# Attention of the second block in units of two heads: weights normalised before the transposes, V stationary in column halves

## The chip, the cores and the metric

The kernel runs on one core of one Trainium2 chip. The metric is the time of one execution on the device in microseconds (us), the median over repeated runs. The engines are TensorE (PE, with its weight loads as PEld), VectorE (DVE), ScalarE (ACT), GpSimd (POOL) and SyncE (SP, which issues the DMAs). Each takes its instructions in the order of its own queue; semaphores hold an instruction back until what it reads or overwrites is ready.

## What is computed

Two blocks of a network over 256 tokens of 1024 channels, in fp32. The first block has two layers of a mixer (mLSTM and dilated attention) and a gated MLP. The second block takes the result as its latents, beside 256 tokens of context; its first layer mixes by attention with 16 heads of 64 channels (4 heads of keys and values, each shared by 4 heads of queries), a window and a sink, its second by gated linear attention. Only this attention matters here:

```python
def softmax_with_sink(s, sink):
    sk = sink.astype(jnp.float32)[None, :, :, None, None]
    m = jnp.maximum(jnp.max(s, axis=-1, keepdims=True), sk)
    e = jnp.exp(s - m)
    return e / (jnp.sum(e, axis=-1, keepdims=True) + jnp.exp(sk - m))
...
        p = softmax_with_sink(jnp.concatenate([s_lat, s_ctx], axis=-1), sink_g).astype(v.dtype)
        return (jnp.einsum('bhgqk,bkhd->bqhgd', p[..., :n_loc], v)
                + jnp.einsum('bhgqk,bkhd->bqhgd', p[..., n_loc:], v_ctx))
```

The latents attend to 256 latent keys (within the window) and 256 keys of the context, 512 in all; the context attends to its own 256 keys. The outputs of all heads, [256, 1024], go through `w_o`.

## The kernel before

Nearly all products are done as three fp32r products of high and low parts (`mm3`, L581; `mm_nat`, L620). The weights come as 591 tiles of [128, 1024], called granules (and 192 more for the adaLN vectors). `ahead` (L453) loads the granules to come (SyncE), makes their high parts `wh` (ScalarE) and low parts `wl` (VectorE), some granules ahead of TensorE. `gran` (L476) does the products of one granule and then one `tick`.

Background work is written as generators. `add` (L501) puts one on a list, with a delay in ticks; `tick` (L508) lets every generator on the list do one step, the oldest first. What a step issues goes into the queues there and then, and the program's order is kept on each engine. So two steps on one engine, in one tick, run in the order of the list, and a step that waits holds up all that stands behind it on its engine. `tick` with main also issues one product of the adaLN vectors (`ada_step`, L549: a multiply and reduction over [128, 1024] on VectorE, its weights loaded by a DMA of 512 KB), if the planner's account says that VectorE is ahead (`late`, L371, below `room`). The account (`Core`, L342) adds for a VectorE instruction 90 ns and its elements a partition divided by 0.96 per ns, and counts TensorE by the columns.

The attention runs in two stages. That of the **context** (`ctx_units`, L1711) runs as background of the first MLP of the first block, whose granules (the loop over `FF` in `layer1`) fill TensorE: 16 units of two heads (h0 and h0 + 2) for one of two query blocks, one unit for every three granules. That of the **latents** (`layer2_attention`, L1804, the loop from L1829) has 32 units of one head, one started at each tick. Eight granules of the context's MLP are put in between, at passes 1, 2, 4, 6, 12, 18, 24 and 30 of the loop; each brings a tick of its own. The last steps of `q_out`, for the last queries, fall into the first ticks.

A unit (`unit`, L1655) has six steps, one a tick, in one bank of PSUM:

1. scores, and the window's mask as a product (TensorE);
2. maximum over the keys and its negation `nm` (VectorE), exponentials `P` with their sum `den` (ScalarE);
3. transposes of P (TensorE); `es`, the sink's share, an addition on VectorE and an exponential on ScalarE;
4. copy of the transposed weights `PT` (ScalarE, or VectorE for every second head of the latents); `den + es` and its reciprocal (VectorE);
5. products with V, PT stationary (128 columns), V moving (64 columns): `aux<-v,PT` or `trb<-v,PT`;
6. the output times the reciprocal into `on` (VectorE for the latents, ScalarE for the context).

For every four heads, `o_out` (L1789) transposes `on` of both blocks (four transposes) and splits the result into high and low parts `oT`, the operand of the product with `w_o` (`aux<-wh,oT` for the latents). The banks of PSUM come from three pools: `mm` (2 banks), `aux` (4), `tr` (2, `trb`); the units of the latents take four of `aux`, then one of `tr`.

Of the kernel before, what the change touches and what calls it, by code (L numbers as in the profile page):

```python
# [18 lines left out]
T = 256  # L19
# [5 lines left out]
# columns of w_in  # L25
# [36 lines left out]
    # streams of the second block: 0 latents, 1 context, 2 both  # L62
# [128 lines left out]
# ------------------------------------------------------------------ small vectors, [128, n]  # L191
# [33 lines left out]
# ------------------------------------------------------------------ constants of the shapes  # L225
# the order of the first block's tokens: token % 4, token % 128 // 4, token // 128
# [33 lines left out]
def rope_tables():  # L260
    """[2, token, 256]: cosines, and sines with the sign of the rotation, for 4 heads of 64."""
# [9 lines left out]
def block2_masks():  # L271
    """window masks of the two query blocks [128, 2, 128], causal masks [128, 4, 128], scan resets [128, 2, 512]"""
# [36 lines left out]
class Views(list):  # L309
    """[128, 256] views of tiles; pair[n]: views 2n and 2n + 1 as one"""  # L310
# [6 lines left out]
class Lazy:  # L317
    """a sequence whose items are worked out when they are asked for"""
# [8 lines left out]
class Costs:  # L327
    """An engine whose instructions are counted in time, roughly"""
# [13 lines left out]
class Core:  # L342
    """The core, with a rough account of how far its tensor and vector engines are (in ns)."""
# [27 lines left out]
    @property  # L371
    def late(self):
        """how much work the vector engine has in front of it"""
        return self.dve - self.pe


class Kernel:
    LOAD, HI, LO, RAWS = 5, 3, 2, 4

    def __init__(self, ctx, tc, i, o):  # L380
# [11 lines left out]
        self.kv, self.on = [None, None], [None, None]  # L392
# [16 lines left out]
    # ---- tiles  # L409
# [25 lines left out]
    def t4x4(self, name, n=8):  # L435
        """n views [128, 2 (hi, lo), 256]; and the tiles [128, 2, 2, 256]"""
# [3 lines left out]
    def t4x8(self, name, n=8):  # L440
        """n views [128, 256]"""
# [3 lines left out]
    # ---- the stream of weights: loads and splits run ahead of the products  # L445
# [7 lines left out]
    def ahead(self, n):  # L453
        """loads, then the high parts, then the low parts of the granules to come"""
# [21 lines left out]
    def gran(self, key, mm, post=None):  # L476
        """One granule: its products, then a step of the background; post runs before the next granule's products."""
# [22 lines left out]
    # ---- background work: generators, one step a granule  # L500
# [34 lines left out]
    # ---- adaLN vectors, channels on partitions  # L535
# [1175 lines left out]
    def ctx_units(self):  # L1711
# [3 lines left out]
        for n, u in enumerate([(b, h0) for h0 in (0, 1, 4, 5, 8, 9, 12, 13) for b in range(2)]):  # L1715
            at = 2 + 3 * n
            self.add(self.unit(self.trb, 1, *u), at)
            if n % 4 == 3:
                self.add(self.o_out(1, n // 4, self.oc, self.trb), at + 8)
# [530 lines left out]
```

## Time and profile before

| | before |
|---|---|
| median of 3 runs | 2144.11 us (2143.8 to 2144.17) |
| profiled execution: span from first to last instruction | 2140.1 us |
| what lies around the span (median less span) | 4.0 us |
| TensorE busy | 2088.5 us, 98% |
| VectorE busy | 1581.5 us, 74% |
| ScalarE busy | 1156.2 us, 54% |
| mean granted TensorE clock | 0.994 of full |

The profile is one execution on the chip. A row of the timeline is: start us, duration us (of all merged ones together), engine, line, operation, output<-inputs by the program's names, shapes, count, and in brackets the idle time before it and what ended that. L338 is the line of a helper that records every instruction of TensorE and VectorE, so tiles tell them apart: `unm` is the unit's `nm`, `uden` its `den`, `ues` its `es`. Matmuls are pipelined, so their durations overlap, and the time that one takes of the engine is read from start to start. An fp32 product stands in the trace as two instructions. The granted clock 1.00 is TensorE's level of 2.4 GHz, 0.50 that of 1.2 GHz.

### The profile page before, as it was taken

The numbers are of one execution on the slowest core, as the hardware profiler recorded it, in microseconds if no ns is written. First come the engines' busy times: TensorE is split into PE (matmuls) and PEld (weight loads), VectorE is DVE, ScalarE is ACT, GpSimd is POOL, SyncE is SP. The second block draws the span as 40 slices with busy tenths as digits, with TensorE's granted clock in tenths as the row PEclk, the third lists the DMA queues.
The fourth block names the chain that finished last, engine by engine and source line by source line (L and its number), as shares of the span: only waits on it lengthen the run. The fifth ranks groups of instructions, "written<-read, shape, count | busy, mean of one in ns | idle before, by whom it ended". The sixth has DMA issues, their size and how long they took to land.

```text
span 2140.1 us, 38280 instructions
## 1 busy us (share of the span) xinstructions
PE 2088.5 (98%) x15192; PEld 1931.2 (90%) x15192; DVE 1581.5 (74%) x2681; ACT 1156.2 (54%) x1972; POOL 44.8 (2%) x62
## 2 busy tenths in 40 slices
PE   7999999999999999999999999999999999999998
PEld 6988999899998998999999998898998989877997
DVE  7778888788887988897899567786664485466555
ACT  5745665555555644666464455555542365445444
POOL 0000000000000000001000000000000010000000
PEclk9999999999999999999999999999999999999999
DMA  8776566688865777554589555304553253214553
GB/s 337 285 287 218 182 215 214 217 286 299 304 243 199 267 278 242 179 190 162 188 296 362 200 179 196 109 31 148 196 189 108 91 182 109 70 60 148 188 187 137
DMA packets 120883, 426.88 MB, mean 199 GB/s; under 512 B 13664, under 2 KB 18528, under 8 KB 120704
## 3 DMA queue, kind: packets, MB, share of 16 engines
q1 hardware_dynamic: 120704, 424.43, 57.0%
q8 instruction: 119, 1.95, 0.4%
q14 instruction: 60, 0.49, 0.1%
HBM read 423.33 MB, written 1.05 MB: 198 GB/s over the span
## 4 chain that ended last, share of the span: by engine, by line
PE 89%; DVE 5%; ACT 4%; issue 1%; DMA 0%; POOL 0%; DVEq 0%; POOLq 0%; SPq 0%; ACTq 0%
PE mm L338 54%; PE aux L338 29%; PE trb L338 5%; ACT wh L464 1%; DVE wl L338 1%; ACT xh L1461 0%; DVE yg L338 0%; ACT u L1499 0%; ACT u L896 0%; DVE hT L338 0%; DMA raw<-in_w 0%; ACT ah L905 0%; POOL rs L667 0%; DVE ee L338 0%; DVE mtmp L338 0%
## 5 line engine op out<-in xcount | busy, mean ns | idle before, releaser
L338 DVE TENSOR_TENSOR wl<-raw,wh 128x1024 fp32r<-128x1024 f32 x591 | 718.7, 1220 | 184.4 <-PE aux L338 72.5
L464 ACT ACTIVATE wh<-raw 128x1024 fp32r<-128x1024 f32 x591 | 623.6, 1059 | 366.5 <-PE mm L338 136.7
L338 PE MATMUL mm<-uT,wh 128*128 128x256 f32 x3488 | 633.2, 283 | 0.0
L338 PEld LDWEIGHTS mm<-uT,wh 128*128 128x128 f32 x3488 | 535.6, 189 | 3.0 <-ACT va L807 0.3
L338 PE MATMUL mm<-uT,wl 128*128 128x256 f32 x1744 | 489.4, 281 | 0.0
L338 PE MATMUL mm<-hT,wh 128*128 128x256 f32 x1888 | 340.5, 282 | 4.0 <-ACT y L1766 2.1
L338 PEld LDWEIGHTS mm<-uT,wl 128*128 128x128 f32 x1744 | 328.9, 189 | 0.0
L338 PEld LDWEIGHTS mm<-hT,wh 128*128 128x128 f32 x1888 | 292.9, 189 | 10.5 <-ACT y L1766 2.3
L338 PE MATMUL mm<-hT,wl 128*128 128x256 f32 x944 | 265.5, 281 | 0.0
L338 DVE CUSTOM_DVE_ANT_0 araw<-araw,silu 128x1024 f32<-128x1024 f32 x192 | 233.1, 1218 | 6.3 <-DMA araw<-in_w 3.8
L338 PE MATMUL aux<-wh,hid 128*128 128x512 f32 x640 | 199.6, 393 | 0.0
L338 PEld LDWEIGHTS mm<-hT,wl 128*128 128x128 f32 x944 | 178.4, 189 | 0.0
L338 PEld LDWEIGHTS aux<-wh,hid 128*128 128x128 f32 x640 | 117.9, 188 | 24.4 <-DVE hid L338 0.2
L338 PE MATMUL aux<-mlg,wh 128*128 128x256 f32 x704 | 129.6, 285 | 0.0
L338 PE MATMUL aux<-wl,hid 128*128 128x512 f32 x320 | 125.4, 392 | 0.0
L338 DVE TENSOR_TENSOR r<-r 128x256 f32<-128x256 f32 (+1 forms) x88 | 39.4, 448 | 116.1 <-ACT r L1899 116.0
L338 PEld LDWEIGHTS aux<-mlg,wh 128*128 128x128 f32 x704 | 109.5, 192 | 0.0
L1899 ACT ACTIVATE r<-mm 128x256 f32<-128x256 f32 (+1 forms) x88 | 35.8, 407 | 124.8 <-PE mm L338 124.8
L338 PE MATMUL aux<-mlg,wl 128*128 128x256 f32 x352 | 99.6, 283 | 0.0
L667 POOL TENSOR_TENSOR rs<-ve,mhalf 128x1 f32<-128x1 f32 (+1 forms) x48 | 41.3, 861 | 2078.0 <-DVE ve L338 1892.5
L338 PE MATMUL mm<-wh,hT 128*128 128x256 f32 (+1 forms) x352 | 78.9, 321 | 0.7 <-DVE qs L338 0.5
L338 DVE CUSTOM_DVE_ANT_0 junk<-araw,silu 128x1024 bf16<-128x1024 f32 x64 | 78.0, 1218 | 0.0
(367 smaller groups left out, 3140.5 us busy)
## 6 DMA issues: line engine op xcount, KB each, us to landing
raw<-in_w SPq DMA_DIRECT2D x591, 512.0 KB, 4.1
araw<-in_w SPq DMA_DIRECT2D x192, 512.0 KB, 5.2
abias<-in_abias SPq DMA_DIRECT2D x32, 192.0 KB, 4.9
xc<-in_ctx SPq DMA_DIRECT2D x4, 512.0 KB, 6.4
x<-in_x SPq DMA_DIRECT2D x2, 512.0 KB, 4.1
gb<-in_ln SPq DMA_DIRECT2D x2, 512.0 KB, 5.7
out_x<-x SPq DMA_DIRECT2D x4, 256.0 KB, 2.0
mk<-in_mmask SPq DMA_DIRECT2D x1, 512.0 KB, 5.5
```

The costliest lines, as they stand in the source:

```text
L338: return f(*a, **k)
L464: nc.scalar.activation(out=wh, in_=self.raws[self.nhi], func=AF.Copy)
L667: nc.gpsimd.tensor_tensor(out=rs, in0=ve, in1=self.mhalf[:, 0:n], op=ALU.pow)
L1899: nc.scalar.activation(out=r[:, 0:n], in_=ps, func=AF.Relu)
```

## The change

The attention of the second block is rewritten in units of two neighbouring heads, for latents and context.

- `weights` (new) does one head of the latents or two of the context: scores; maximum, exponentials and now also the sink's exponential, straight from `nm` on ScalarE; then, in a step of its own, `den + es`, reciprocal and the scaling of P (in place, on VectorE, 512 columns); then the transposes; then the copy of PT, always on ScalarE.
- `unit` runs `weights` for both heads, for the latents with the second head one tick behind the first one. Then come the products with V for both: V stationary (64 columns), PT moving (128 columns), the first head's output in partitions 0 to 63 of the bank, the second head's in 64 to 127. A last step splits this output, which is now transposed, straight into `oT`, 128 columns a unit.
- `o_out`, `on` and their transposes are gone.
- The units of the latents start at every second tick; their two banks come from `aux`, `aux`, `tr` in turn.

The rest of the diff takes out comments and empty docstrings.

```diff
+    def weights(self, bank, st, b, heads, res):
...
+        for n in range(step):
+            nc.scalar.activation(out=es[:, n:n + 1], in_=sink[:, n:n + 1], func=AF.Exp, bias=nm[:, n:n + 1])
+        yield
+        nc.vector.tensor_tensor(out=den, in0=den, in1=es, op=ALU.add)
+        nc.vector.reciprocal(out=den, in_=den)
+        for n in range(step):
+            c = slice(n * w, (n + 1) * w)
+            nc.vector.tensor_scalar(out=P[:, c], in0=P[:, c], scalar1=den[:, n:n + 1], scalar2=None, op0=ALU.mult)
         yield
         for k in range(4):
             nc.tensor.transpose(sc[:, k * 128:(k + 1) * 128], P[:, k * 128:(k + 1) * 128], self.ident)
-        nc.vector.tensor_tensor(out=es, in0=sink, in1=nm, op=ALU.add)
-        nc.scalar.activation(out=es, in_=es, func=AF.Exp)
         yield
         PT = self.t2("PT")
-        if st or h0 % 2:
-            nc.scalar.activation(out=PT, in_=sc, func=AF.Copy)
+        nc.scalar.activation(out=PT, in_=sc, func=AF.Copy)
+        res.append((sc, PT))
+
+    def unit(self, bank, st, b, h0, oT, made):
...
+        if st:
+            yield from self.weights(bank, st, b, heads, res[0])
+            yield
         else:
-            nc.vector.tensor_copy(out=PT, in_=sc)
-        nc.vector.tensor_tensor(out=den, in0=den, in1=es, op=ALU.add)
-        nc.vector.reciprocal(out=den, in_=den)
-        yield
-        for n, h in enumerate(heads):
-            vs = slice((h // 4) * 64, (h // 4) * 64 + 64)
-            vals = [kv[s]["v"][:, k, vs] for s in range(st, 2) for k in range(2)]
-            for k, v in enumerate(vals):
-                c = (n * len(vals) + k) * 128
-                nc.tensor.matmul(sc[:, n * 64:n * 64 + 64], PT[:, c:c + 128], v, start=k == 0, stop=k == len(vals) - 1)
-        yield
-        on = self.on[st][b]
-        for n, h in enumerate(heads):
...
+            parts = [self.weights(bank, st, b, [h], r) for h, r in zip(heads, res)]
+            next(parts[0])
+            yield
+            while not res[1]:
+                for p in parts:
+                    next(p, None)
+                yield
+        o = res[0][0][0][:, 0:128]
+        vs = slice((h0 // 4) * 64, (h0 // 4) * 64 + 64)
+        vals = [kv[s]["v"][:, k, vs] for s in range(st, 2) for k in range(2)]
+        for k, v in enumerate(vals):
+            for n in range(2):
+                PT, c = (res[0][0][1], (n * 2 + k) * 128) if st else (res[n][0][1], k * 128)
+                nc.tensor.matmul(o[n * 64:n * 64 + 64], v, PT[:, c:c + 128], start=k == 0, stop=k == len(vals) - 1)
+        yield
...
+        self.split(t[:, 0, bs], t[:, 1, bs], o)
...
     def layer2_attention(self, x, xc):
-        pools = (self.aux,) * 4 + (self.trb,)
-        left = [(0, b, hq) for hq in range(16) for b in range(2)]
-        for n, u in enumerate(left):
-            self.add(self.unit(pools[n % len(pools)], *u), n)
-            if n % 8 == 7:
-                self.add(self.o_out(0, n // 8, oT, self.trb), n + 7)
+        pools = self.aux, self.aux, self.trb
+        for n, u in enumerate([(b, h0) for h0 in range(0, 16, 2) for b in range(2)]):
+            self.add(self.unit(pools[n % 3], 0, *u, oT, made), 2 * n)
```

## Rows read from the trace of the kernel before

**Rows 1.** The first two parts of the page: busy time of the engines (share of the span, instructions), and TensorE's busy share in 40 slices of the span, in tenths.

```profile
PE 2088.5 (98%) x15192; PEld 1931.2 (90%) x15192; DVE 1581.5 (74%) x2681; ACT 1156.2 (54%) x1972; POOL 44.8 (2%) x62
...
PE   7999999999999999999999999999999999999998
```

**Rows 2.** Windows: stretch, its length, busy time of PE, PEld, DVE, ACT and POOL in it (instructions), granted clock, DMA share, GB/s. First from the context's stage, then from the latents'.

```profile
460.00:480.00 20.00, 20.00 (x172) 20.00 (x171) 18.18 (x36) 11.76 (x26) 0.00 (x0) 1.00 0.94 332
...
1402.00:1412.00 10.00, 10.00 (x80) 9.46 (x79) 8.67 (x30) 5.61 (x15) 0.00 (x0) 1.00 0.14 52
```

**Rows 3.** Timeline of TensorE in the latents' stage: transposes of P, scores, transposes of `on`, V products, transposes of P; a granule (from 1419.80 to 1422.61); the first output product.

```profile
1416.47 0.61 PE L338 MATMUL trb<-ident,P 128*128 128x128 f32 x4
1416.83 0.48 PE L338 MATMUL aux<-kT,qT 128*128 128x256 f32 x2
...
1417.50 0.60 PE L338 MATMUL trb<-ident,on 128*128 128x128 f32 x4
1417.94 1.00 PE L338 MATMUL aux<-v,PT 128*128 128x64 f32 x8
1418.78 0.61 PE L338 MATMUL aux<-ident,P 128*128 128x128 f32 x4
...
1419.80 0.63 PE L338 MATMUL mm<-wh,hid 128*128 128x512 f32 x2
...
1422.61 0.55 PE L338 MATMUL trb<-v,PT 128*128 128x64 f32 x4
...
1450.72 0.71 PE L338 MATMUL aux<-wh,oT 128*128 128x512 f32 x2
```

**Rows 4.** Timeline of VectorE, then of ScalarE, in the latents' stage, with nothing left out between the rows of either.

```profile
1408.36 0.69 DVE L338 TENSOR_REDUCE umx<-aux 128x1 f32<-128x512 f32 x1 [0.40 <-PE aux L338]
1409.08 0.16 DVE L338 SCALAR_TENSOR_TENSOR unm<-umx,nsink 128x1 f32<-128x1 f32 x1
1409.20 0.28 DVE L338 TENSOR_SCALAR on<-aux,uden 128x64 f32<-128x64 f32 x1
1409.40 0.15 DVE L338 TENSOR_TENSOR uden<-uden,ues 128x1 f32<-128x1 f32 x1
1409.58 0.17 DVE L338 RECIPROCAL uden<-uden 128x1 f32<-128x1 f32 x1
...
1409.36 0.69 ACT L1681 ACTIVATE P<-aux,unm 128x512 f32<-128x512 f32 x1 [0.45 <-DVE unm L338]
1409.94 0.19 ACT L1681 ACTIVATION_READ_ACCUMULATOR P<-aux,unm 128x1 f32 x1
1410.04 0.59 ACT L1691 ACTIVATE PT<-aux 128x512 f32<-128x512 f32 x1
1410.51 0.20 ACT L1687 ACTIVATE ues<-ues 128x1 f32<-128x1 f32 x1
```

**Rows 5.** Products of the second layer with a stationary operand of 64 columns (128*64), outputs in halves of the partitions: timeline of TensorE, and the weight loads of all of them (min, median and max ns).

```profile
1854.60 1.09 PE L338 MATMUL aux<-gS,gqk 128*64 128x256 f32 x8
1855.62 1.13 PE L338 MATMUL aux<-gv,ATm 128*128 128x256 f32 x4
1856.68 0.66 PE L338 MATMUL aux<-gS,gqk 128*64 128x256 f32 x4
...
L338 PEld LDWEIGHTS aux<-gS,gqk x64: 132/136/137, 1854.6 to 1919.7; 128*64 128x64 f32 x64
```

**Rows 6.** Timeline of TensorE around the V products of a unit of the context.

```profile
456.93 1.00 PE L338 MATMUL trb<-v,PT 128*128 128x64 f32 x8
457.73 0.48 PE L338 MATMUL aux<-mlg,wh 128*128 128x256 f32 x2
458.06 0.28 PE L338 MATMUL aux<-mlg,wl 128*128 128x256 f32 x1
458.17 0.40 PE L338 MATMUL aux<-mlg,wh 128*128 128x256 f32 x2
```

**Rows 7.** Groups of instructions by line, engine, operation, tiles and shape, count | busy us, mean ns | idle before: scalings by a column from SBUF to SBUF, and a copy of 128 columns on ScalarE.

```profile
L338 DVE TENSOR_SCALAR gon<-gon,rs 128x256 f32<-128x256 f32 x8 | 2.4, 348 | 0.8 <-POOL rs L667 0.8
L338 DVE TENSOR_SCALAR xh<-x,rs 128x1024 f32<-128x1024 f32 x8 | 6.0, 752 | 3.8 <-POOL rs L667 3.8
...
L1338 ACT ACTIVATE mD<-aux,gc 128x128 f32<-128x128 f32 x16 | 5.5, 362 | 0.3
```

**Rows 8.** The last adaLN products (by tile: min, median and max ns, first and last start), and the window behind them.

```profile
L338 DVE CUSTOM_DVE_ANT_0 araw<-araw,silu x4: 1217/1218/1219, 1172.2 to 1180.7; 128x1024 f32<-128x1024 f32 x4
...
1180.00:1200.00 20.00, 20.00 (x172) 20.00 (x171) 13.14 (x18) 8.95 (x12) 0.00 (x0) 1.00 0.55 184
```

**Rows 9.** The start of the latents' stage: timeline of VectorE, then a piece of the chain of waits (start us, us, what).

```profile
1361.60 0.68 DVE L338 TENSOR_REDUCE umx<-aux 128x1 f32<-128x512 f32 x1
...
1362.39 1.35 DVE L338 TENSOR_TENSOR rp<-qn,rope 128x512 f32<-128x512 f32 x3
...
1368.01 0.76 DVE L338 TENSOR_TENSOR qs<-qr,qs 128x256 fp32r<-128x256 f32 x2 [1.53 <-ACT qs L650]
...
1367.67 0.31 ACT qs L650
```

**Rows 10.** Timeline of TensorE with the idle time there, and a window of the latents' stage (granted clock third from the end).

```profile
1374.21 0.66 PE L338 MATMUL trb<-ident,qs 128*128 128x128 f32 x4 [1.56 <-ACT qT L1653]
...
1372.00:1382.00 10.00, 8.44 (x50) 7.58 (x49) 5.16 (x17) 5.13 (x13) 0.00 (x0) 0.83 0.16 54
```

More of the change, by code (lines that the diff above doesn't have):

```diff
@@ L391, in __init__ @@
         self.filler = iter(())
-        self.kv, self.on = [None, None], [None, None]
+        self.kv = [None, None]
         self.mix_filler = [self.ctx_qkv, self.ctx_in]
@@ L1653, in q_out @@
                 nc.scalar.activation(out=out, in_=src, func=AF.Copy)
-    def unit(self, bank, st, b, h0):
+    def weights(self, bank, st, b, heads, res):
         nc = self.nc
         kv = self.kv
-        step = 1 + st
-        heads = [h0 + 2 * n for n in range(step)]
+        step = len(heads)
         w = 512 // step
         bs = slice(b * 128, b * 128 + 128)
-        sink = self.V("sink")[:, h0:h0 + 2 * step - 1:2]
+        cs = slice(heads[0], heads[0] + step)
+        sink = self.V("sink")[:, cs]
         sc = bank()
@@ L1677, in unit @@
         nc.vector.tensor_reduce(out=mx, in_=sc.rearrange("p (a b) -> p a b", a=step), axis=AX.X, op=ALU.max)
-        nc.vector.scalar_tensor_tensor(out=nm, in0=mx, scalar=-1.0, in1=self.nsink[:, h0:h0 + 2 * step - 1:2], op0=ALU.mult, op1=ALU.min)
+        nc.vector.scalar_tensor_tensor(out=nm, in0=mx, scalar=-1.0, in1=self.nsink[:, cs], op0=ALU.mult, op1=ALU.min)
         P = self.t2("P")
@@ L1695, in unit @@
-        nc.vector.reciprocal(out=den, in_=den)
-        yield
-        for n, h in enumerate(heads):
-            vs = slice((h // 4) * 64, (h // 4) * 64 + 64)
-            vals = [kv[s]["v"][:, k, vs] for s in range(st, 2) for k in range(2)]
-            for k, v in enumerate(vals):
-                c = (n * len(vals) + k) * 128
-                nc.tensor.matmul(sc[:, n * 64:n * 64 + 64], PT[:, c:c + 128], v, start=k == 0, stop=k == len(vals) - 1)
-        yield
-        on = self.on[st][b]
-        for n, h in enumerate(heads):
-            if st:
-                nc.scalar.activation(out=on[:, h * 64:h * 64 + 64], in_=sc[:, n * 64:n * 64 + 64], func=AF.Copy, scale=den[:, n:n + 1])
-            else:
-                nc.vector.tensor_scalar(out=on[:, h * 64:h * 64 + 64], in0=sc[:, n * 64:n * 64 + 64], scalar1=den[:, n:n + 1], scalar2=None, op0=ALU.mult)
@@ L1711, in ctx_units @@
-    def ctx_units(self):
-        self.on[1] = [self.t4("on", (128, 1024)) for _ in range(2)]
-        self.oc = [None] * 8
[L1715 to L1719, printed above, removed]
+        nc.scalar.activation(out=PT, in_=sc, func=AF.Copy)
+        res.append((sc, PT))
+    def unit(self, bank, st, b, h0, oT, made):
+        nc = self.nc
+        kv = self.kv
+        heads = [h0, h0 + 1]
+        res = [[], []]
+        if st:
+            yield from self.weights(bank, st, b, heads, res[0])
+            yield
+        else:
+            parts = [self.weights(bank, st, b, [h], r) for h, r in zip(heads, res)]
[12 more added lines that the diff above has]
+                nc.tensor.matmul(o[n * 64:n * 64 + 64], v, PT[:, c:c + 128], start=k == 0, stop=k == len(vals) - 1)
+        yield
+        j = h0 // 2
+        if made[j // 2] is None:
+            made[j // 2] = self.t4("oT", (128, 2, 2, 256), F32R)
+        t = made[j // 2][:, j % 2]
+        bs = slice(b * 128, b * 128 + 128)
+        self.split(t[:, 0, bs], t[:, 1, bs], o)
+        if b == 1:
+            oT[j] = t
@@ L1721, in ctx_out @@
+    def ctx_units(self):
+        self.oc, made = [None] * 8, [None] * 4
+        for n, u in enumerate([(b, h0) for h0 in range(0, 16, 2) for b in range(2)]):
+            self.add(self.unit(self.trb, 1, *u, self.oc, made), 2 + 3 * n)
     def ctx_out(self):
@@ L1787, in tokens @@
         return lambda k, hl, b: a[k][:, hl, b * 128:(b + 1) * 128]
-    def o_out(self, st, j2, oT, bank):
-        nc = self.nc
-        on = self.on[st]
-        tr = bank()
-        for jj in range(2):
-            for b in range(2):
-                c = (j2 * 2 + jj) * 128
-                nc.tensor.transpose(tr[:, jj * 256 + b * 128:jj * 256 + b * 128 + 128], on[b][:, c:c + 128], self.ident)
-        yield
-        t = self.t4("oT", (128, 2, 2, 256), F32R)
-        nc.scalar.activation(out=t[:, :, 0], in_=self.pair(tr), func=AF.Copy)
-        nc.vector.tensor_tensor(out=t[:, :, 1], in0=self.pair(tr), in1=t[:, :, 0].bitcast(F32), op=ALU.subtract)
-        oT[2 * j2], oT[2 * j2 + 1] = t[:, 0], t[:, 1]
     def layer2_attention(self, x, xc):
@@ L1817, in layer2_attention @@
         self.flush()
-        self.on[0] = [self.t4("on", (128, 1024)) for _ in range(2)]
-        oT = [None] * 8
-        pools = (self.aux,) * 4 + (self.trb,)
-        left = [(0, b, hq) for hq in range(16) for b in range(2)]
-        for n, u in enumerate(left):
-            self.add(self.unit(pools[n % len(pools)], *u), n)
-            if n % 8 == 7:
-                self.add(self.o_out(0, n // 8, oT, self.trb), n + 7)
+        oT, made = [None] * 8, [None] * 4
+        pools = self.aux, self.aux, self.trb
+        for n, u in enumerate([(b, h0) for h0 in range(0, 16, 2) for b in range(2)]):
+            self.add(self.unit(pools[n % 3], 0, *u, oT, made), 2 * n)
         other = self.mlp_out(1, 1, self.hid_c, self.yc, self.mmb)
```

## The prediction

> **What bounds the kernel now.** Read first the busy line and the slices: TensorE is busy 98% of a span of 2140.1 us, VectorE 74%, ScalarE 54%, and TensorE's row of slices is all nines but for the first and last slice [rows 1]. So what the change takes from TensorE's queue is gained, unless another engine then ends last. The change lies in two stages, so the windows come next [rows 2]. In the context's stage (440 to about 620 us, between the granules of the first MLP) TensorE is busy 20.00 us of 20 and VectorE about 18. In the latents' stage (1358 to 1451 us) TensorE is full from 1402 us on, with VectorE at 8.7 us of 10, ScalarE at 5.6. The order of the queues says why. A tick of the latents' stage on TensorE is V products 0.84 us, transposes 0.36, scores and mask 0.67, 1.87 us a head, one right behind the other [rows 3]; VectorE waits for it (0.40 us ahead of a reduction) [rows 4]. The stage ends where the output product starts, at 1450.72 [rows 3].
>
> **The change, TensorE.** The transposes of `on` go: 32, four of them 0.44 us [rows 3], 16 in each stage, 1.75 us a stage. The V products get V as the stationary operand, 64 columns wide, in halves of the array. 128 columns of fp32 stream in 0.11 us (the transposes), 256 then in 0.22. The nearest row is gS<-gqk: eight half-wide products of 256 columns, 1.76 us one after the other, took 1.02 [rows 5], so two halves run side by side. Entering and leaving that form costs about 0.3 us together: eight of them and four full-wide ones, 8 x 0.22 = 1.76 us with the halves paired, took 1.02 + 1.06. A unit of the latents then has 8 pairs of 128 columns: 8 x 0.11 + 0.3 = 1.18 us for two heads, where 2 x 0.84 = 1.68 stand now; bounds 0.88 (no switching) and 1.76 (no pairing). A unit of the context has 4 pairs: 0.44 + 0.3 = 0.74 us. Now it takes 0.80, and the second product behind it starts 0.09 late (0.33 us for two, where one takes 0.11 to 0.12) [rows 6], 0.89; the gain is 0.15 a unit, 2.4 us for 16 (bounds 0 and 7).
>
> The Trainium skill ("TensorE: Matmul & The Clock Gate", Part 3) speaks against this part: weight loads overlap running matmuls only when the row group differs, and the halves here share their rows. By that rule a pair would cost its load and its stream. The gS rows contradict it: eight loads of 0.136 us and eight streams lie within 1.02 us [rows 5].
>
> **The context's stage.** TensorE gains 1.75 + 2.4 = 4.2 us. VectorE: out go `es` (0.15), and a quarter of the 0.69 us split of `oT`; in come two scalings of 256 columns, 0.35 each [rows 7], and a 128-column split, about 0.28: +0.66 us a unit, 10.6 us. The planner counts that (two scalings of 357 ns, one split of 223 by its formula, less `es` and the old split: +0.69 us a unit) and puts off some 9 adaLN products of 1.22 us instead. These ended at 1180.7 us with TensorE full and VectorE at 13 of 20 us in the next window [rows 8]; so they and their loads of 512 KB land there at no cost; if that cover were gone, 9 x 1.22 = 11 us. The new wait (the sum of the weights, on VectorE, one granule behind ScalarE's exponentials) has behind it an adaLN product and a split of weights, 2.4 us, in which the 1.1 us of exponentials end. Nothing else is late: **-4.2 us**.
>
> **The latents' stage, where I see the trouble.** Call a head's steps S (scores), M (maximum on VectorE, exponentials on ScalarE), N (sum, reciprocal and scaling of P on VectorE), T, C (copy of the transposes), V. Before, the reciprocal is two ticks behind M and touches only the output. Now N is in the tick right behind M and T waits for it. Units start every second tick with their heads one tick apart, older units first, so every tick puts on VectorE: N of one head, then the maximum of the next. N waits for the exponentials of the tick before; behind it in the same queue stands the maximum that the next exponentials wait for. That is a ring with one head in it: maximum, exponentials, N, maximum. From rows, start to start: reduction 0.72, negation to the start of the exponential 0.28, exponential 0.58, its sum 0.10, the sink's exponential 0.20, addition 0.18, reciprocal 0.20 [rows 4], and 0.03 from ScalarE's end to VectorE's start [rows 9]. The scaling of 512 columns has no row; 256 take 347 ns and 1024 take 753 [rows 7], so about 0.48, of which the last 0.08 overlap the next instruction as in [rows 4]: 0.40 (bounds 0.27 and 0.67, by those two rows). Sum 2.69 us a head, against 1.87 + 0.4 of granules now. In every second tick the split of an older unit stands ahead of N: its ScalarE half waits behind the exponentials (128 columns, about 0.33 by the 362 ns of mD [rows 7]), its VectorE half 0.20 more: 0.44 once the overlap is off.
>
> What hides in the ring's waits: wl (1.22 us, in the 1.2 us while VectorE waits for the exponentials), wh, both PT copies (2.69 - 0.89 = 1.8 us of each round are free on ScalarE), the 2.81 us granules (TensorE's share is 1.18 + 2 x 1.04 = 3.3 us a pair of heads and 0.8 of granules, 4.1 of 5.8), and the scores of a unit's second head, which wait for a bank until an older unit's outputs are split. What does not: the rotations of the last queries (1.35 us for three of four instructions, about 2.0), and their splits, for which VectorE waits 1.5 us [rows 9], some 2.5 us beyond the wait; a wh of 1.05 ahead of the split twice, 1.9; the additions to y, 0.8. So from the first reduction at 1361.60 [rows 9]: 1.91 to the first N, 31 x 2.69 = 83.4, 13 x 0.44 = 5.7, extras 5.2: the last N begins at 1457.8. Then N 0.9, T 0.5, C 0.6, V 1.2, the last granule 2.8: the output product starts at 1463.8, not 1450.72, **+13.1 us**. The 16 x 0.50 + 1.75 = 9.75 us that TensorE sheds here are off the path.
>
> **The clock.** Up to 1374.21 TensorE idled 1.56 us, and the mean granted clock of 1372 to 1382 is 0.83, which is 3.4 us at the lower level, 1.2 GHz (0.17 x 10 / 0.5) [rows 10]. TensorE will now idle some 1.7 us of every 5.8 (two heads, 2 x 2.69 + 0.44). Half the clock doubles 4.1 us a pair to 8.2, but only while it lasts, and the ring leaves TensorE slack. Bounds 0 and +15 us; I take +2, nearest to the one dip shown: 3.4 us at half the clock do the work of 1.7, of which the ring hides part.
>
> **The sum.** Span 2140.1 - 4.2 + 13.1 + 2 = 2151.0; the profiled span is 4.0 us below the median of the runs, 2144.1, so 2155.
>
> **Rivals.** *The ring does not bind* (faster). If the engines slip against each other as they do now, TensorE sets the pace: 9.75 us off in this stage, 4.2 in the other, 2130.1. It decides where a head's ring is below TensorE's 2.05 us (4.1 a pair); 2.3 us would make it even. For it: VectorE's own work, 1.6 to 1.9 us a head, is below 2.05, and TensorE is the bound now. Against: the waits are in a fixed order, and the terms are read off running queues. *Ring and gain cancel*: terms of the ring 0.3 us too large (a cheaper scaling, less of the extras), 2140 to 2148. *The clock stays low* for half of the stage: TensorE needs 6.2 us a pair beside a ring of 5.8 and each holds the other up, +8 to +15 more, 2162 to 2172. *The halves do not pair* (the change does not do what it says): the context's 2.4 us are lost, the latents hang on the ring, 2157.4. *Loads of the halves are not hidden*: a pair takes 0.136 + 0.11 us, a context unit 4 x 0.25 + 0.3 = 1.3, 0.4 more than now, 16 x 0.55 = 8.8 us above my sum; a latents' unit 2.3, still beside the ring: 2163.9. (That is the rule of Part 3 above.) *The put-off adaLN products collide*: up to +11, 2166.
>
> **How the numbers follow.** The ring as summed (with the halves pairing or not): 0.53, 2148 to 2162. Clock or adaLN on top: 0.15, to 2172; loads not hidden 0.02. Cancel: 0.10. Ring does not bind: 0.20, 2126 to 2140. 0.2% (4.3 us) is about what a measurement of this kernel tells from no change: faster 0.20, same 0.10, slower 0.70. The range from 2131 to 2168 leaves out about 0.1 at either end.
>
> **What would show it.** In the latents' stage of the changed kernel: VectorE idle about 1.1 us ahead of the additions to `uden`, released by ScalarE's `ues`, some 30 times; reductions 2.7 and 3.1 us apart in turn; TensorE idle ahead of the transposes of P, released by VectorE; half-wide products two at a time. In the context's stage: no idle TensorE, fewer adaLN products, the end of the stage some 4 us earlier. I am wrong if TensorE stays full in the latents' stage, or if reductions come closer than 2.3 us on the mean.

## The result

The changed kernel takes 2164.95 us, median of 4 runs (2164.16 to 2166.53), against 2144.11: ratio 1.0102, 95% interval 1.009 to 1.0115, so slower by 20.8 us. The forecast was 2155.0, in a range of 2131 to 2168. The direction, the mechanism and its pace were right; the loss is about twice the forecast one of 10.9 us.

The profiled execution has a span of 2164.7 us (before: 2140.1). The page of the changed kernel, busy line and two rows of slices (compare [rows 1]):

```profile
PE 2095.1 (97%) x15160; PEld 1919.6 (89%) x15160; DVE 1589.3 (73%) x2673; ACT 1164.0 (54%) x1996; POOL 44.6 (2%) x62
...
PE   7999999999999999999999999889999999999998
...
PEclk9999999999999999999999999899999999999999
```

The row of all nines has got two eights, at 1353 to 1461 us, and the clock's row one in the same stretch: the latents' stage. Windows of the changed kernel (columns: busy us of each engine, then granted clock, DMA share, GB/s):

```profile
1180.00:1200.00 20.00, 20.00 (x171) 20.00 (x170) 18.19 (x28) 8.81 (x11) 0.00 (x0) 1.00 0.94 343
1362.00:1372.00 10.00, 7.48 (x38) 5.63 (x36) 7.21 (x20) 4.45 (x11) 0.00 (x0) 0.82 0.17 58
1372.00:1382.00 10.00, 6.78 (x22) 5.61 (x23) 5.47 (x14) 5.30 (x13) 0.00 (x0) 0.50 0.14 53
1402.00:1412.00 10.00, 6.86 (x46) 5.45 (x45) 6.25 (x19) 5.65 (x18) 0.00 (x0) 0.84 0.01 2
1462.00:1472.00 10.00, 8.21 (x44) 6.15 (x45) 3.56 (x10) 4.20 (x10) 0.00 (x0) 0.60 0.16 51
```

The first row is the context's part: the adaLN products that were put off fill 1180 to 1200, VectorE 18.2 us where 13.1 stood [rows 8], and TensorE stays full beside them. In 1402 to 1412 no engine is full: TensorE 6.9 us of 10 (before 10.00 [rows 2]), VectorE 6.3, ScalarE 5.7. Each engine waits for another. VectorE's timeline there (start, duration, instruction, idle time before it and what ended that):

```profile
1404.07 0.68 DVE L338 TENSOR_REDUCE umx<-aux 128x1 f32<-128x512 f32 x1
1404.79 0.16 DVE L338 SCALAR_TENSOR_TENSOR unm<-umx,nsink 128x1 f32<-128x1 f32 x1
1406.04 0.16 DVE L338 TENSOR_TENSOR uden<-uden,ues 128x1 f32<-128x1 f32 x1 [1.09 <-ACT ues L1684]
1406.23 0.16 DVE L338 RECIPROCAL uden<-uden 128x1 f32<-128x1 f32 x1
1406.43 0.48 DVE L338 TENSOR_SCALAR P<-P,uden 128x512 f32<-128x512 f32 x1
1406.84 0.68 DVE L338 TENSOR_REDUCE umx<-aux 128x1 f32<-128x512 f32 x1
1407.55 0.16 DVE L338 SCALAR_TENSOR_TENSOR unm<-umx,nsink 128x1 f32<-128x1 f32 x1
1408.99 0.29 DVE L338 TENSOR_TENSOR oT<-aux,oT 128x128 fp32r<-128x128 f32 x1 [1.28 <-ACT oT L650]
1409.20 0.15 DVE L338 TENSOR_TENSOR uden<-uden,ues 128x1 f32<-128x1 f32 x1
...
1409.98 0.68 DVE L338 TENSOR_REDUCE umx<-aux 128x1 f32<-128x512 f32 x1
```

This is the ring as forecast: maximum, a wait of 1.09 us for the exponentials, N, next maximum; 2.77 us later in this pair and 3.14 where a split stands ahead of N (forecast 2.69 and 3.13). Those two spacings alternate from the seventh maximum to the last, but for three longer ones of 4.1. In two of these a split of weights (`wh`) stands ahead of the high half on ScalarE; in the third (1412.74 to 1416.89) a unit's V products stand behind a granule on TensorE:

```profile
1410.57 1.05 PE L338 MATMUL mm<-wh,hid 128*128 128x512 f32 x2
...
1414.45 1.09 PE L338 MATMUL trb<-PT,v 128*64 128x128 f32 x16
```

The start and the end are where the forecast is off. VectorE at the start of the stage, from the first maximum on:

```profile
1359.94 0.68 DVE L338 TENSOR_REDUCE umx<-aux 128x1 f32<-128x512 f32 x1
...
1367.53 0.76 DVE L338 TENSOR_TENSOR qs<-qr,qs 128x256 fp32r<-128x256 f32 x2 [1.99 <-ACT qs L650]
...
1378.66 0.69 DVE L338 TENSOR_REDUCE umx<-trb 128x1 f32<-128x512 f32 x1 [0.74 <-PE trb L338]
1379.39 0.16 DVE L338 SCALAR_TENSOR_TENSOR unm<-umx,nsink 128x1 f32<-128x1 f32 x1
1384.40 0.29 DVE L338 TENSOR_TENSOR oT<-aux,oT 128x128 fp32r<-128x128 f32 x1 [4.85 <-ACT oT L650]
```

The wait of 4.85 us goes back to TensorE, in the same execution:

```profile
1378.42 1.05 PE L338 MATMUL mm<-wh,hid 128*128 128x512 f32 x2
...
1382.63 0.39 PE L338 MATMUL mm<-wl,hid 128*128 128x512 f32 x1
1382.95 1.09 PE L338 MATMUL aux<-PT,v 128*64 128x128 f32 x16
```

A granule takes 4.5 us (2.81 in [rows 3]) because the clock is at its lower level, 1.2 GHz, until 1382; the first unit's V products stand behind it, the split behind those, and on VectorE N and the next maximum behind the split. The last maximum (VectorE), then TensorE at the end:

```profile
1461.99 0.68 DVE L338 TENSOR_REDUCE umx<-aux 128x1 f32<-128x512 f32 x1
...
1462.22 0.63 PE L338 MATMUL aux<-ident,P 128*128 128x128 f32 x4 [1.08 <-DVE P L338]
...
1464.65 1.97 PE L338 MATMUL trb<-PT,v 128*64 128x128 f32 x14 [1.44 <-ACT PT L1696]
1466.55 1.12 PE L338 MATMUL aux<-ident,P 128*128 128x128 f32 x4
1467.60 2.78 PE L338 MATMUL aux<-PT,v 128*64 128x128 f32 x16
1470.31 1.22 PE L338 MATMUL mm<-wh,hid 128*128 128x512 f32 x2
...
1474.96 0.63 PE L338 MATMUL aux<-wh,oT 128*128 128x512 f32 x2
```

From the last maximum (1461.99) to the output product it is 13.0 us, with V products of 2.7 us and a granule of 4.65, again at the lower level (0.60 in the window); the forecast had 7.9.

### The profile page after: what moved, and what is told of

It reads as the page before. It is cut to its first block, busy times and chain, and to the rows that moved or that the text cites. A ratio compares the mean times of both kernels' runs of the same rounds, so it can differ in the third digit from the quotient of the medians.

```text
span 2164.7 us, 38194 instructions
## 1 busy us (share of the span) xinstructions
PE 2095.1 (97%) x15160; PEld 1919.6 (89%) x15160; DVE 1589.3 (73%) x2673; ACT 1164.0 (54%) x1996; POOL 44.6 (2%) x62
## 4 chain that ended last, share of the span: by engine, by line
PE 85%; DVE 7%; ACT 5%; issue 1%; DMA 0%; POOL 0%; ACTq 0%; DVEq 0%; POOLq 0%; SPq 0%
PE mm L338 54%; PE aux L338 27%; PE trb L338 4%; DVE wl L338 1%; ACT wh L464 1%; DVE umx L338 1%; ACT P L1681 1%; DVE P L338 1%; DVE uden L338 0%; ACT xh L1461 0%; ACT u L896 0%; DVE yg L338 0%; ACT u L1499 0%; DMA raw<-in_w 0%; DVE hT L338 0%
```

## The experiments

Ratios are to the kernel before, run beside it on the same chip (medians of it 2142.65 to 2144.02). N is the sum, reciprocal and scaling of a head; a granule is one of the eight of the context's MLP between the latents' units.

**1. Maximum ahead of N.** N is put in a list that the tick runs at its end; the latents' instructions are the same, in another order.

```diff
-        nc.vector.tensor_tensor(out=den, in0=den, in1=es, op=ALU.add)
...
+        def norm():
+            nc.vector.tensor_tensor(out=den, in0=den, in1=es, op=ALU.add)
...
+        if st:
+            norm()
+        else:
+            self.ends.append(norm)
         yield
```

In `tick`, behind the steps of all generators:

```diff
+        for f in self.ends:
+            f()
+        self.ends = []
```

> The changed kernel, with the same instructions in another order: in each tick of the latents' stage the sum, reciprocal and scaling of a head (N) are issued behind the next head's maximum, not ahead of it. Theory (ring): maximum, exponentials, N, next maximum no longer follow one another for each head; TensorE sets the pace at about 3.9 us a pair of heads (2 x 1.03 us of scores and transposes, 1.03 of half-wide V products, 0.8 of granules) in place of 5.9, the low clock goes with the waits, and the stage gives back 25 to 37 us: 2128 to 2140 us, the output product at about 1438 to 1450, reductions 2.0 to 2.3 us apart on the mean, VectorE's wait for ues gone. Rival (the half-wide V products and the low clock at the ends of the stage are what costs): the order hardly matters, 2158 to 2166. Rival (VectorE's own work, 1.6 to 1.9 us a head, is the next bound and its waits stay): 2140 to 2150.

2139.01 us, ratio 0.9979 (0.997 to 0.9988): 26 us back by order alone, 4 of them at the end (9.0 us in place of 13.0), so the ring with the clock that it costs is the loss. VectorE in the steady part:

```profile
1423.26 0.29 DVE L338 TENSOR_TENSOR oT<-aux,oT 128x128 fp32r<-128x128 f32 x1 [0.49 <-ACT oT L653]
1423.46 0.68 DVE L338 TENSOR_REDUCE umx<-aux 128x1 f32<-128x512 f32 x1
1424.18 0.16 DVE L338 SCALAR_TENSOR_TENSOR unm<-umx,nsink 128x1 f32<-128x1 f32 x1
1424.26 0.15 DVE L338 TENSOR_TENSOR uden<-uden,ues 128x1 f32<-128x1 f32 x1
1424.44 0.16 DVE L338 RECIPROCAL uden<-uden 128x1 f32<-128x1 f32 x1
1424.64 0.49 DVE L338 TENSOR_SCALAR P<-P,uden 128x512 f32<-128x512 f32 x1
```

The wait ahead of the sum is gone; maxima come 1.58 and 2.36 us apart, 3.94 a pair, with 2.1 to 3.3 at granules; with the start they are 2.55 apart on the mean of the stage, where 2.0 to 2.3 was expected. The wait of 0.49 us for a split's high half is what is left.

**2. and 3. One stage alone.** The unit, the output transposes and the call of the kernel before serve the other stage.

> The change in the context's stage alone; the latents' attention is that of the kernel before. Theory: TensorE is the bound there and sheds 1.75 us of transposes and about 2 us of V products: 2139.5 to 2142.5 us (4.2 us by the forecast, 1.6 by what is left of it in the changed kernel when the latents' stage begins). Rival (the context's part is lost elsewhere, to the adaLN products that it puts off or to the clock): 2143.5 or more.

> The change in the latents' stage alone; the context's attention is that of the kernel before. Theory: the whole loss is here, 25 us by the trace of the changed kernel: 2166 to 2170 us. Rival (the stage is late because the context's part moved work into it): below 2160.

Context alone 2139.85, 0.9989 (0.9979 to 0.9999); latents alone 2165.51, 1.01 (1.0085 to 1.0115). The context's gain is 3.7 us by the medians (forecast 4.2), but the ten runs of 2 lie between 2139.27 and 2144.96, and the interval leaves room for 0.2 to 4.5. The whole loss is the latents'; its time is just below the expected range.

**4. Scores twice.**

```diff
-        for n, h in enumerate(heads):
+        for n, h in [e for e in enumerate(heads) for _ in range(2 - st)]:
             lhs = kv[st]["q"][h // 4][:, h % 4, bs]
```

> The changed kernel, with the score products of every latents' head issued twice over (the second time over the first, the same sums): 0.67 us a head, 21 us of TensorE work more, on an engine that waits for VectorE. Theory (ring, with the low clock at the start and the end of the stage on top): TensorE has 5.2 us of work in 5.9 a pair, so the ring's pace of 2.76 and 3.15 us stays; the busier engine keeps the full clock over more of the stage and the start and the end give back 3 to 10 us: 2155 to 2163. Ring, with the clock as a bystander: 2164 to 2168. Rival (TensorE's time counts, waits come and go): 21 us on top or a good part of them, 2175 to 2186.

2162.97, 1.0088 (1.0073 to 1.0103): 21 us of TensorE work more, and no more time. The pattern stays at 2.76 and 3.15; the granted clock is 1.00 from 1382 on, and the end takes 9.0 us (1461.60 to 1470.58) in place of 13.0. The start is no shorter: spacings of 5.47, 5.20 and 6.53, where the changed kernel has 5.47, 4.14 and 6.73.

**5. and 6. A later start.** Experiment 6 is the changed kernel with this edit, 5 has the order of 1 as well.

```diff
-            self.add(self.unit(pools[n % 3], 0, *u, oT, made), 2 * n)
+            self.add(self.unit(pools[n % 3], 0, *u, oT, made), 2 * n + 4)
-            if n in (1, 2, 4, 6, 12, 18, 24, 30):
+            if n in (1, 2, 3, 4, 16, 22, 28, 34):
```

> The order of e1_max_first, and beside it the first units of the latents begin four ticks later, with the first four granules of the context's MLP (2.8 us each at the full clock) in the four iterations ahead of them and the later four granules as far behind the units as before. In e1 the first six maxima lay 22.3 us apart in all, where 3 pairs of 3.95 us and two granules would be 17.5; TensorE idled beside the rotations and splits of the last queries, and its clock fell. Theory (those steps stand in the engines' queues among the first units'): the granules cover them, 4 to 8 us less than e1: 2131 to 2135 us. Rival (the start is bound by the queries' own chain of steps, which is no shorter): 2137 to 2142.

> The changed kernel with that later start alone; its ring stays. Its first nine spacings of maxima were 8.5 us longer than the ring's pattern by the trace (3.59, 5.47, 4.15, 6.73 us where 2.76 and 3.15 are the pattern), where the forecast had 2.5. Theory (the start of the stage is the mis-sized term): 4 to 8 us less than the changed kernel: 2157 to 2161 us, with the pattern of 2.76 and 3.15 from the third maximum on. Rival (the first units are slow by themselves): 2163 to 2167.

5: 2134.09, 0.9957 (0.9943 to 0.9972), as expected. 6: 2163.09, 1.0088 (1.0071 to 1.0105), where 2157 to 2161 was expected. In 6 the pattern does hold from the third maximum on, and first to last maximum is 93.7 us in place of 102.05; but the first maximum comes at 1366.30 in place of 1359.94, since two more granules (5.6 us), which stood among the units, are now ahead of it. The collisions of the start are real, 8.3 us; only the cover was not free.

**7. No scaling.** The loop over the scalings runs over `range(step if st else 0)`.

> The changed kernel without the scaling of the latents' weights by the reciprocal (left out: the attention of the latents is not normalised). Theory (ring): the scaling holds VectorE 0.40 us, start to start, in each head's round, and the round is the stage's pace, so maxima come 2.36 and 2.75 us apart and 31 x 0.40 = 12.4 us go: 2151 to 2154 us, a little less if the clock dips less. Rival (the wait for the exponentials takes the place of the scaling, because ScalarE or TensorE ends last): 2160 to 2166.

2146.68, 1.0016 (1.0006 to 1.0025). Maxima 2.25 and 2.61 apart: a round is 0.51 to 0.54 us shorter, since the scaling's wait for the reciprocal goes too. 31 x 0.52 is 16 us, and the clock, 1.00 from 1382 on, gives the end back. One term of the ring taken out shortens every round, so ring it is; the miss is that I counted 0.40.

**8. V products not in turn.**

```diff
-        for k, v in enumerate(vals):
-            for n in range(2):
+        for n in range(2):
+            for k, v in enumerate(vals):
```

> The changed kernel with the half-wide V products of a unit in another order: all of the first head, then all of the second, where they stood in turn. Theory (halves run side by side only when neighbours in the queue take different column halves): a context unit streams 8 x 0.11 where 4 x 0.11 stood, 0.44 us more, and the context's stage is bound by TensorE: 16 x 0.44 = 7 us more; the latents hang on the ring and hide theirs: 2169 to 2173 us, and a block of V products of the latents takes 1.8 to 2.1 us in place of 1.03. Rival (the halves do not run side by side now, or the engine finds the partner further down the queue): 2164 to 2167 and no change of the block.

2159.80, 1.0077 (1.0062 to 1.0092), below the range of either theory. Latents, not in turn, then the changed kernel, in turn (the starts of the transposes behind them are 1457.12 and 1457.27):

```profile
1455.60 1.58 PE L338 MATMUL aux<-PT,v 128*64 128x128 f32 x16
1457.12 0.66 PE L338 MATMUL aux<-ident,P 128*128 128x128 f32 x4
```

```profile
1456.24 1.09 PE L338 MATMUL aux<-PT,v 128*64 128x128 f32 x16
1457.27 0.66 PE L338 MATMUL aux<-ident,P 128*128 128x128 f32 x4
```

1.52 us and 1.03: the order matters there, and the latents hide it. In the context a unit's block takes 0.59 us from its start to that of the next instruction in either order, so there it does not, and the 7 us never came. The starts of the single instructions, not in turn, say more. The 16 of a latents' block fall into two rows of eight, 0.11 us apart within a row; the second row begins 0.49 us into the block, 0.006 us behind the fifth start of the first. In the context (two rows of four) it begins 0.01 us behind the first start. The trace does not name the heads; read as first and second head, a product starts beside one of the other half that stands four places ahead of it in the queue, and the latents' 0.49 us are the first four, alone. That the kernel became faster goes with the clock: 1.00 in 1462 to 1472, and an end of 9.0 us.

**9. A granule behind the V products.** `if n in (1, 2, 5, 6, 13, 19, 25, 31):` in the changed kernel: five of the eight granules move by one pass.

> The changed kernel with six of its eight granules of the context's MLP one iteration later or earlier, so that a granule stands behind a unit's V products in TensorE's queue and not right ahead of them. In the changed kernel the first unit's V products stand behind a granule that takes 4.5 us at half the clock; the first split waits for them, and with it everything behind the split in VectorE's queue: a spacing of maxima of 6.73 us in place of 3.15. Theory (that granule holds the ring): the spacing falls to 3.2 to 4 us and the kernel takes 2 to 4 us less: 2161 to 2163.5 us. Rival (the wait moves to the next granule): 2164 to 2167.

2159.49, 1.0077 (1.0064 to 1.009), below the expected range. VectorE at the first split:

```profile
1381.04 0.29 DVE L338 TENSOR_TENSOR oT<-aux,oT 128x128 fp32r<-128x128 f32 x1 [1.06 <-ACT oT L650]
```

1.06 us of waiting in place of 4.85; the spacings of 4.14 and 6.73 are 3.08 and 4.08, 3.7 us together. The end is 11.3 us in this execution, with a granted clock of 0.70 in 1462 to 1472 (0.60 in the changed kernel).

**10. to 12.** 10 is 5 with the later granules at 17, 23, 29 and 35. 11 is the kernel before with the edit of 5 (units at `n + 4`, output transposes at `n + 11`). 12 is 5 with the edit of 8.

> The order and the later start of e5_max_first_late, with the four later granules one iteration further, behind a unit's V products. Theory (a split that waits for a granule holds VectorE for 0.7 to 1.7 us, four times): 1 to 3 us less than e5, 2131 to 2133 us. Rival (TensorE is the bound, 9.5 us of 10, and the order of its work is all one): 2133.5 to 2135.

> The kernel before with the later start alone (its units four ticks later, the first four granules ahead of them): what of e5's gain is not the change's. TensorE idles 1.56 us and loses 1.7 us to the low clock at the start of the stage in the kernel before. Theory (the start costs both kernels much the same): 3 to 5 us less than before, 2139 to 2141 us, so that the change in its other order is worth some 5 to 7 us. Rival (only the changed kernel's order collides there): 2143 to 2145.

> e5_max_first_late with the V products of a unit not in turn: all of the first head, then all of the second, 1.51 us a block where 1.02 us stand in turn (the two as measured in the latents' stage of e8_not_in_turn and of the changed kernel). Theory (without the ring TensorE sets the pace of the latents' stage): all of 16 x 0.49 = 7.8 us come on top of e5: 2140 to 2143 us. Rival (VectorE and the splits still set it, or half of it): 2134 to 2138.

10: 2132.92, 0.9951 (0.9937 to 0.9964), not to be told from 5, and the fastest version tried. 11: 2137.00, 0.997 (0.9958 to 0.9982), more than the 3 to 5 us expected: the start costs the kernel before as much, so more than half of 10's gain is not the change's. 12: 2135.93, 0.9964 (0.995 to 0.9977), 1.8 us more than 5 where TensorE as the bound would give 7.8, and not to be told from 5. Its pattern is 1.58 and 2.36 as in 5. So the pace of 3.94 is not TensorE's, though there is no more room: from 1382 to 1432 TensorE is busy 10.00 us of 10 in 12. VectorE in 5:

```profile
1384.20 0.29 DVE L338 TENSOR_TENSOR oT<-aux,oT 128x128 fp32r<-128x128 f32 x1 [0.49 <-ACT oT L653]
1384.41 0.68 DVE L338 TENSOR_REDUCE umx<-aux 128x1 f32<-128x512 f32 x1
...
1388.15 0.29 DVE L338 TENSOR_TENSOR oT<-trb,oT 128x128 fp32r<-128x128 f32 x1 [0.49 <-ACT oT L653]
```

Between these rows VectorE waits only there: 3.45 us of work and 0.49 of wait a pair.

**13. and 14. The split's low half last.** The low half goes into a list that the tick runs behind N; 13 in the changed kernel, 14 in 10.

```diff
-        self.split(t[:, 0, bs], t[:, 1, bs], o)
+        hi, lo = t[:, 0, bs], t[:, 1, bs]
+        nc.scalar.activation(out=hi, in_=o, func=AF.Copy)
+        low = lambda: nc.vector.tensor_tensor(out=lo, in0=o, in1=hi.bitcast(F32), op=ALU.subtract)
+        if st:
+            low()
+        else:
+            self.lows.append(low)
```

> The changed kernel with one move: the low half of a split (VectorE) is issued at the end of its tick, behind the next maximum, not at the tick's head. Theory (the split is a term of the ring, since VectorE waits there for its high half on ScalarE): the spacing of 3.15 us falls to 2.76, 15 x 0.39 = 5.9 us, and where a granule or a split of weights delayed the split (6.73, 4.1 us) up to 6 us more: 2153 to 2160 us. Rival (the banks, which come free with the split, hold the scores back by as much): 2163 to 2167.

> e10_both (maximum first, later start, granules behind the V products) with the low half of the split last in its tick as well. In e5 a pair of heads takes 3.94 us, 3.45 of VectorE's work and 0.49 of its wait for the split's high half, and the pattern stayed at 3.94 with 0.49 us more on TensorE. Theory (VectorE with that wait is the bound once the ring is broken): up to 0.49 us a pair less, 3 to 7 us: 2126 to 2130 us. Rival (TensorE and the banks are as late; 9.6 us of 10 busy): 2131.5 to 2134.

13: 2160.87, 1.0084 (1.0068 to 1.0099), just above the expected range. The spacings are 2.76 and 2.78, so the split's 0.39 us is a term of the ring; but some rounds are longer (5.71, 4.16), and the start is as it was (4.14, 6.60). 14: 2143.72, 0.9999 (0.9991 to 1.0008): the theory fell. TensorE in 14:

```profile
1385.41 0.47 PE L338 MATMUL aux<-kT,qT 128*128 128x256 f32 x2 [1.62 <-DVE oT L338]
...
1390.49 0.48 PE L338 MATMUL trb<-kT,qT 128*128 128x256 f32 x2 [1.62 <-DVE oT L338]
```

The bank comes free with the low half, and the scores of a second head, which wait for it, are now 1.62 us late: 5.09 us a pair. The rival had named the banks, but priced them at 2131.5 to 2134.

**15. Scores four times** in the heads 0 and 1, twice in the others.

> The changed kernel with the score products issued four times over for the first four heads and twice for all others: TensorE is given work where it idles at the start of the stage (1.9, 2.3 and 1.0 us) and its clock falls. Theory (the low clock is 3 us of the start's excess, the queues the rest): full clock from 1362 to 1392, the spacing of 6.73 us down to 4.5 to 5.5 us, the spacing of 5.47 as it is, the end as in e4: 2158 to 2161 us. Rival (the start is order alone): the spacings stay and 2162 to 2165.

2163.61, 1.0097 (1.0083 to 1.011). Its windows:

```profile
1372.00:1382.00 10.00, 7.64 (x46) 6.89 (x46) 5.83 (x15) 4.75 (x11) 0.00 (x0) 0.83 0.17 55
1462.00:1472.00 10.00, 8.18 (x73) 6.34 (x73) 4.99 (x13) 5.09 (x14) 0.00 (x0) 1.00 0.16 52
```

With a granted clock of 0.83 in 1372 to 1382 in place of 0.50 the start is no shorter: spacings of 5.48, 5.21 and 6.04, and 27.3 us for the first six in place of 25.5 (the scores themselves add to some). So a higher clock alone does not mend the start. The end is 9.0 us again (1463.24 to 1472.22).

**16. and 17.** 16 is 11 with the context's part of the change. 17 is 14 with the low half between the maximum and N.

> The change in the context's stage alone, with the later start of e11_before_late: the latents' attention is that of the kernel before. Theory (the two add up, and the latents' part of the change is worth nothing even in its best order so far): 2137.0 - 3.7 = 2133.3, so 2132 to 2134.5 us, the time of e10_both. Rival (the latents' part in e10 is worth some us): 2135 or more.

> e14_all_three with the low half of a split between the next maximum and N, where e10_both has it ahead of the maximum and e14 behind N. Theory (VectorE's wait of 0.49 us for the high half is what sets 3.94 us a pair in e10, the bank held 1.6 us too long what set 5.1 in e14): the high half is ready when the maximum is done, VectorE does not wait, the bank comes free 0.3 us later than in e10: 3.45 to 3.7 us a pair, 4 to 8 us less than e10 over 16 pairs less what the granules take back: 2126 to 2130 us. Rival (the banks hold the scores back still): 2132 to 2140.

16: 2136.96, 0.997 (0.9958 to 0.9981), in the rival's range. With the later start the context's part shows no gain by the medians (11 has 2137.00), and 10 is some 4 us faster than either; the intervals of 10 and 16 still overlap a little. The profiled executions do not put those 4 us into the latents' stage. The output product starts, in 10, 16 and 11:

```profile
1442.89 0.62 PE L338 MATMUL aux<-wh,oT 128*128 128x512 f32 x2
1443.10 0.71 PE L338 MATMUL aux<-wh,oT 128*128 128x512 f32 x2
1445.96 0.71 PE L338 MATMUL aux<-wh,oT 128*128 128x512 f32 x2
```

At that point 16 is 2.9 us ahead of 11, and 10 only 0.2 ahead of 16; from the first maximum it is 77.4 us in 10 and 78.4 in 16. What follows is the same work in all kernels here, and it takes 688.3 us in 10, 690.8 in 16, and 688.2 to 691.3 in the profiled executions of this case. So the latents' part in its best order is worth about 1 us by the traces and 4 by the medians, and is not shown to be worth more than nothing. 17: 2136.20, 0.9968 (0.9956 to 0.998): its pair is 4.29 us; VectorE no longer waits for the high half, but TensorE still idles 0.83 us ahead of a second head's scores. The profile puts that wait down to the instruction right behind the low half; 14 and 17 together point to the bank, whose wait then takes the place of that for the high half.

## Why the forecast was right in sign and half in size

By its own steps, in spans (2164.7 measured, 2151.0 forecast, 13.7 apart):

| step | forecast us | measured us |
|---|---|---|
| first maximum, against [rows 9] | -4.2 | -1.7 |
| first to last maximum | 94.3 | 102.05 |
| of this, ring and splits, 31 rounds | 89.1 | 91.4 |
| of this, extras | 5.2 | 10.6 |
| last maximum to output product | 7.9 | 13.0 |
| clock, held apart | 2 | in the rows above |
| behind the output product | 0 | +0.4 |

- **The ring** held: 2.76 and 3.15 us where 2.69 and 3.13 were summed. Experiments 1 and 7 show it as the cause, and 13 shows the split in it. The wait for `ues` stands there 13 times (12 of 1.09 us, one of 0.49), not 30: in the other rounds the split's wait or a split of weights takes its place.
- **The step that failed** is the size of two terms. One is "extras 5.2": the prediction lists the granules among what hides in the ring's waits, and gives the last queries' steps 2.5 us. The first six spacings are 25.5 us, 7.7 over the pattern. Of these, 3.7 go when the granule ahead of the first V products, which holds the split and so the ring, is put behind them (9); the other 4.0 stand against the 2.5. One more granule ahead of V products costs 1.0 (1412.74 to 1416.89). The two splits of weights cost 1.9, as forecast, and the 0.8 for `y` do not show in the spacings. The other is "the clock, +2", taken from one dip: the ring leaves TensorE idle, the clock falls at both ends of the stage, and at the end nothing hides it. The end is 13.0 us, and 9.0 wherever the clock was full there (4, 8, 15), so 4 us in that one place. The other 1.1 over the 7.9 is the sum's own: at the full clock, too, the last block of V products takes 1.83 us and not 1.2.
- **The context's stage** gives almost what was forecast, and more than half of that is lost again on the way to the latents. Just behind the stage TensorE is 3.8 us ahead (forecast 4.2), at 1280 us still 3.1, at 1300 only 1.5: in between the clock dips to 0.84, where the kernel before has 1.00, and 0.16 of 10 us is the 1.6 lost (rows below the list). In 1 and 2 a dip at 1000 to 1010 is deeper instead (0.68 and 0.72, before 0.83) and takes 1.2 to 1.3. So "nothing else is late" failed mainly by the clock, outside the attention. The V block is 0.59 us, start to start; with the 0.09 that it starts late and the 0.10 that the second product behind it is late it costs 0.78, where 0.74 was forecast and 0.89 stood before. The adaLN products moved as said: 51 of the form that writes `araw` in 440 to 640 became 44, and four of the other form none (forecast some 9 fewer), and TensorE is full where they land.
- **Halves in pairs**: right. A block of the latents is 1.03 us, start to start, and 1.18, as forecast, with the 0.10 that it starts late behind a granule and the 0.05 that the transposes behind it are late. Eight products lie in it with their loads, so the rival of loads that are not hidden did not come true. The Trainium skill ("TensorE: Matmul & The Clock Gate", Part 3), by which loads overlap running products only where the row group differs, does not agree with that 1.03 us: on the same rows, 16 loads of 0.137 us lie within it.
- **"The ring does not bind", 2130.1**: without the ring the kernel takes 2139, not 2130. TensorE's 9.75 us do not appear. In the steady part VectorE's work and its wait for the split set 3.94 a pair (5, 12), and when that is relieved, the banks come next (14, 17); the start costs 5 more (1 against 5). I had priced that rival by TensorE alone; how the rest of the 9.75 is lost is not worked out.
- **"The clock stays low for half of the stage"**: 2162 to 2172 holds the measured time, but not for its reason: in the middle of the stage the pattern stays, at 0.83 (1442 to 1452) and 1.00 (1452 to 1462) alike.

The products behind the context's stage (min, median and max ns, first and last start), before and changed; then the window of the changed kernel with the dip:

```profile
L338 PE MATMUL aux<-mlg,wh x352: 279/283/366, 447.3 to 654.2; 128*128 128x256 f32 x176
L338 PE MATMUL aux<-mlg,wh x352: 279/283/364, 447.3 to 650.4; 128*128 128x256 f32 x176
...
1290.00:1300.00 10.00, 7.92 (x44) 7.16 (x43) 6.63 (x11) 6.26 (x12) 0.00 (x0) 0.84 0.50 166
```

What stays open: how the 4.0 us that 9 leaves at the start divide between the queue's order and the clock (15 filled the idle time with work that itself delays maxima); whether the latents' part gains anything in its best order; and why the same work behind the output product takes 688 us in one execution and 691 in another, as much as the gains in question.

## What to carry to other kernels

When a step of one item is moved ahead in an in-order queue, write the queue down for two items: if the next item's first step stands behind a wait for this item's last, the pipeline is one item deep, whatever the busy shares say, and swapping two groups of instructions can give it back (26 us here). Price the start and the end of such a stage apart from its pace, with the clock at which a waiting TensorE will do them, and look which granule stands ahead of a product that the ring waits for. And before a wait is moved behind other work, ask which buffer it frees: the low half at the tick's end cost some 10 us (10 against 14).

## What the runs showed of the hardware

- More TensorE work in no more time: 21 us more in experiment 4, 16 x 0.49 = 7.8 us more in 8, with ratios of 1.0088 and 1.0077 beside 1.0102. Where the engine idled less, the granted clock at the end of the stage was 1.00 in place of 0.60.
- Half-wide products run side by side even when they are not neighbours in the queue. Head by head, a context's block of 2 x 4 instructions takes 0.59 us as in turn; a latents' block of 2 x 8 takes 1.52 in place of 1.03. By the single starts the second half begins beside the product four places ahead of it, in both (experiment 8).
- Loads of half-wide products are hidden: 16 of 0.137 us lie within the 1.03 us of a latents' block (changed kernel).
